# Five modulation vectors as fp32 TensorE products in four column groups, and the first mixer's low parts on one engine

## The chip, the cores and the metric

One NeuronCore of a Trainium2 chip runs the whole program in one launch. The metric is the device time of that launch in microseconds (us), the median of several executions. The engines are TensorE (PE in the profile, its weight loads PEld), VectorE (DVE), ScalarE (ACT), GpSimd (POOL) and SyncE (SP), which here issues nearly all DMAs.

## What is computed

Two transformer blocks in fp32, one behind the other, on 256 tokens of width 2048. What matters here is how a conditioning vector `c` enters: in each block it gives six modulation vectors of 2048 elements (shift, scale and gate for the mixer and for the feed-forward part).

```python
def first_block(x, c, w_ada, b_ada, ...):
    c_act = jax.nn.silu(c)
    mod = c_act @ w_ada[l] + b_ada[l]
    sh_m, sc_m, gt_m, sh_f, sc_f, gt_f = jnp.split(mod[:, None, :], N_MOD, axis=-1)
    h = rmsnorm(x, pre_mix_norm[l]) * (1.0 + sc_m) + sh_m
    proj = h @ w_in[l]
    o_hg = hgrn2_group(...)
    o_gdn = gdn_group(...)
    y = jnp.concatenate([o_hg, o_gdn], axis=-1) @ w_out[l]
    x = x + gt_m * rmsnorm(y, post_mix_norm[l])
    h = rmsnorm(x, pre_ffn_norm[l]) * (1.0 + sc_f) + sh_f
    y = jnp.square(jax.nn.relu(h @ w_ff1[l])) @ w_ff2[l]
    x = x + gt_f * rmsnorm(y, post_ffn_norm[l])
```

`w_ada` is 2048 x 12288 in fp32, so its product with one row is a matter of reading 100 MB for each block. The second block has the same frame with an attention mixer of four kinds and a gated feed-forward part.

## The kernel before

**The stream of weights.** All weight matrices come from HBM in tiles of 512 KB (128 partitions x 1024 fp32), in one list, `items`, in the order in which they are used. `dma_to` issues the DMAs on SP into a ring of `raw` tiles: 5 of them, and 3 more during the prologue. `prep` takes the next item of the list when the planner says so.

**GEMM items.** Products are made at fp32 precision from fp32r parts. ScalarE copies a raw tile to a high part `wh`, and VectorE or GpSimd subtracts it to get the low part `wl` (`low.tensor_tensor` in `prep`; `l_eng` and the item's mark `"low"`, set from the table `LOW`, choose the engine). TensorE then multiplies high x high, high x low and low x high, 12 or 24 products for a tile. There are 4 pairs of `wh`/`wl` (6 in some places), so prepared tiles wait for TensorE there.

**Modulation items.** An item with `"ada"` holds 128 x 1024 elements of `w_ada`: two blocks of 128 rows for one vector, or one block of rows for two vectors. VectorE multiplies each half by the column of `csil` (silu of `c`, one value per partition) and adds it to `acc`, 128 x 512, one instruction for each half:

```python
dve.scalar_tensor_tensor(a, w, sc, a, op0=MUL, op1=ADD)
```

After all 16 row blocks `acc` holds 128 partial sums per column. `col_gen` sums them over the partitions on TensorE, either with four products with `ones`, or with four transposes and four accumulating ScalarE copies, and makes the columns `A` and `B` of a norm. `row_gen` makes a row of a gate with two products with `ones_r`. Vectors 0 and 1 of block 1 (shift and scale of its mixer) are the first things the program needs.

**The order.** The program is written instruction by instruction, in an order that a planner (`_Clock`, with a price for each kind of instruction) works out while it writes; each engine runs its own instructions in that order. `fill`, called after each pair of weight and operand, puts in steps of the generators of the mixer (`fillers`, `pri`, `urgent`) and calls `prep` for the next item if the clock says that its data are there.

**The stages.** A prologue reads the weights of vectors 0 and 1 for the first 512 columns. Then come the eight "wide" blocks of the input product (`hq, hf, hv, hg, zq, zk, zv, gg`, first half of the heads) in three passes over a quarter of the operand each, since each quarter needs its own 512 columns of `A` and `B`. Six of the eight blocks go through two banks of PSUM from the pool `mx` in each pass (`mbanks`) and are added up in SBUF. Then the rest of the input product runs, with the HGRN2 and delta-rule generators in between, and the output product `oA`, `oB`; the feed-forward part; and block 2. The weights of the other modulation vectors are spread between the GEMM items by `weight(k)`. PSUM has eight banks: four for GEMM (`g`), four for everything else (`mx`).

Of the kernel before, what the change touches and what calls it, by code (L numbers as in the profile page):

```python
# [74 lines left out]
class _Clock:  # L75
    """Estimates, while the program is written, when each engine gets to what it is given (us)."""
# [25 lines left out]
    def cost(s, eng, op, out, ins):  # L102
# [3 lines left out]
        if eng == "pe":  # L106
            if op == "transpose":
                return max(n, 128) * 0.417e-3 * 2
            if ins[0].dtype == FR:
                return n * 0.417e-3 * (1 if n >= 256 else 4) + 2.5e-3  # L110
            return 4 * 0.417e-3 * max(n, 128)
# [45 lines left out]
class _Eng:  # L157
    """An engine whose instructions pass through the clock."""
# [18 lines left out]
def two_blocks(ctx, tc, I, out):  # L177
# [57 lines left out]
    def add_ada(blk, v, q, kp, fin, row):  # L235
        items.append({"ada": (blk, v, q, kp), "fin": fin, "row": row})

    def dma_to(n):
        while st["d"] < min(n, len(items)) and rslots:
# [5 lines left out]
            if "ada" in it:  # L245
# [3 lines left out]
                if kp == 0:  # L249
                    for _ in range(40):  # L250
                        if len(accs) + len(vs) > 4:
                            fill_step(True, urgent)
# [16 lines left out]
    def prep(low=None):  # L269
# [9 lines left out]
        if "ada" in it:  # L279
            blk, vs, q, kp = it["ada"]  # L280
            for k in range(2):
# [28 lines left out]

    held = {}
# [23 lines left out]
    def prep_at():  # L335
        """When the data and the place of the next item are there."""
# [172 lines left out]
    def run_last(parts, done, script=()):  # L509
        """Ends of blocks, the first token tile ahead of the second: (block, banks, units)."""  # L510
# [24 lines left out]
    def run_first(b, script, last=False):  # L535
        """A block of kind S at the start of a phase, the first token tile ahead of the second."""
# [122 lines left out]
    def col_gen(blk, v, q):  # L659
# [3 lines left out]
        if blk == 0 and v < 2:  # L663
# [47 lines left out]
    def ada_vecs(blk, vs, key=None, mul=False):  # L711
        n = 8 * len(vs)
        for q in range(4):
            for kp in range(n):
# [6 lines left out]
                ADA.append((blk, vs, q, kp, fin, key is not None))  # L721

# [84 lines left out]
    def turn(post, name):  # L807
        """Steps between two phases: residual sum and norm, (first token tile before the other)."""
# [16 lines left out]
    # =====================================================================  # L825
    # plan of the blocks
    # =====================================================================
# [12 lines left out]
    # ---- evacuations, block 1  # L840
# [80 lines left out]
    # ---- log decay and beta of the delta rule  # L921
# [39 lines left out]
    # ---- gated, normalised heads to the transposed operand  # L961
# [28 lines left out]
    # ---- HGRN2, four heads  # L990
# [56 lines left out]
    # ---- gated delta rule, four heads of one half of the tokens  # L1047
# [153 lines left out]
    # ---- plan of block 1  # L1201
# [107 lines left out]
    # operand tiles of the output product: 0-3, 4-7 first half of the groups, see quad()  # L1309
# [62 lines left out]
    # ---- block 2: evacuations of the input product  # L1372
# [26 lines left out]
    # ---- attention: scores, bias, maximum, exponential and its sum  # L1399
# [155 lines left out]
    # ---- NSA  # L1555
# [142 lines left out]
    # ---- differential attention  # L1698
# [140 lines left out]
    # ---- the modulation's rows come in between, ahead of their uses  # L1839
    ada_vecs(0, (0, 1))  # L1840
    n_first = len(ADA)
    ada_vecs(0, (3, 4))
    ada_vecs(0, (2,), "gt_m", True)
# [10 lines left out]
    def weight(k):  # L1854
        if k[0] in ("oB", "pB") or k == "fv" or k[1:] == (0, 0) and k[0] in ("f1", "ga") or k in (("f1", 0, 1), ("f2", 3, 2), ("f2", 3, 3)):
            return 0.0
        if k == "ab" or k[1] == 0 and k[0] in ("zq", "zk", "zv", "gg", "hq", "hf", "hv", "hg"):
            return 0.3
        if k[0] == "oA":
            return 2.0  # L1860
        if k in ("qG", "kvH", "sv"):
            return 0.5
        if k in (("hq", 1), ("hf", 1)):
            return 0.6
# [148 lines left out]
    while any(it.get("rs", (0,))[0] >= RAW_BUFS for it in items[st["p"]:st["d"]] if "raw" in it):  # L2013
        assert prep()
# [296 lines left out]
```

## Time and profile before

| | us |
|---|---|
| runs of the kernel before | 2861.53, 2865.45, 2865.94 |
| median of the runs | 2865.45 |
| span of the profiled execution (its own time, none other is shown) | 2873.1 |
| TensorE busy | 2634.5 (92%) |
| VectorE busy | 2060.7 (72%) |
| ScalarE busy | 1243.8 (43%) |
| GpSimd busy | 729.0 (25%) |

The mean granted clock of TensorE over the span is 0.959 of 2.4 GHz. The shares are means over stages with different limits, so the rows below are taken by stage: the prologue (0 to 38 us), the three passes of the wide blocks (38 to 249), the rest of the first mixer with `oA` (249 to 790), the turn to the feed-forward part (790 to 857). Nearly all instructions stand on one line of the program, that of the helper `call`, so groups are told apart by the names of their tiles: `acc<-raw,csil,acc` is a multiply-add of a modulation item, `wl<-raw,wh` a low part. An fp32 product of two fp32 operands leaves two records on TensorE.

### The profile page before, as it was taken

To read this page: it belongs to the slowest core of one execution; us is meant where nothing else is said; L and a number is where in the kernel's file an instruction comes from. 1 tells how busy PE (TensorE), PEld (TensorE's weight loads), DVE (VectorE), ACT (ScalarE), POOL (GpSimd) and SP (SyncE) were. 2 spreads that over 40 slices of the span, in tenths; PEclk is the share of its full clock that TensorE was granted. 3 is DMA by queue.
4 is the path that set the end of the run, shared out by engine and by line. 5 is a ranking of instruction groups with operands and counts; after the bars stand their busy time and mean duration, and the time that the engine had idled before them with its cause. 6 is when DMAs were issued, how large, how long until landed. Compare 5 with 4: busy or idle time off the path is not lost.

```text
span 2873.1 us, 43930 instructions
## 1 busy us (share of the span) xinstructions
PE 2634.5 (92%) x17089; PEld 2386.7 (83%) x17089; DVE 2060.7 (72%) x2449; ACT 1243.8 (43%) x2011; POOL 729.0 (25%) x401
## 2 busy tenths in 40 slices
PE   4788889888979999999998899998879999999998
PEld 4778868867869798897997798886669989998997
DVE  7897988899678877778755548678766665554456
ACT  3333343343454444444444436454454444443343
POOL 4663465653130000000002474554520000000001
PEclk9888999889989999999999899999989999999999
DMA  9787566567748988988865675667747777656664
GB/s 319 236 280 193 158 219 198 162 206 239 244 147 271 319 293 291 310 272 303 296 212 166 180 223 168 189 215 249 242 157 228 232 240 229 191 184 191 184 184 146
DMA packets 346593, 643.88 MB, mean 224 GB/s; under 512 B 31488, under 2 KB 50640, under 8 KB 344976
## 3 DMA queue, kind: packets, MB, share of 16 engines
q1 hardware_dynamic: 343296, 628.26, 68.4%
q10 hardware_dynamic: 2336, 10.42, 1.0%
q8 instruction: 134, 2.20, 0.3%
q0 software_dynamic: 752, 2.39, 0.2%
q14 instruction: 75, 0.61, 0.1%
HBM read 636.27 MB, written 4.19 MB: 223 GB/s over the span
## 4 chain that ended last, share of the span: by engine, by line
PE 49%; DVE 8%; DMA 6%; ACT 3%; issue 3%; POOL 2%; SPq 0%; ACTq 0%; POOLq 0%; DVEq 0%
PE g L167 47%; DMA raw<-in_w_ff_dram 5%; DVE acc L167 2%; PE mx L167 2%; DVE wl L167 2%; ACT wh L167 2%; POOL wl L167 1%; DMA raw<-in_ada_w_dram 1%; DVE xres L167 1%; POOL y L167 1%; DVE S L167 0%; DVE hTl L167 0%; ACT hTh L167 0%; DVE v L167 0%; ACT sq L167 0%
## 5 line engine op out<-in xcount | busy, mean ns | idle before, releaser
L167 ACT ACTIVATE wh<-raw 128x1024 fp32r<-128x1024 f32 (+2 forms) x817 | 846.6, 1045 | 1072.0 <-PE g L167 554.7
L167 DVE TENSOR_TENSOR wl<-raw,wh 128x1024 fp32r<-128x1024 f32 (+1 forms) x601 | 751.2, 1256 | 487.5 <-ACT wh L167 479.2
L167 PE MATMUL g<-hTh,wh 128*128 128x256 f32 x3328 | 961.0, 289 | 5.3 <-ACT wh L167 2.5
L167 PE MATMUL g<-hTh,wl 128*128 128x256 f32 x3328 | 950.8, 286 | 6.5 <-POOL wl L167 5.0
L167 PE MATMUL g<-hTl,wh 128*128 128x256 f32 x3328 | 949.3, 285 | 0.3 <-DVE hTl L167 0.3
L167 DVE SCALAR_TENSOR_TENSOR acc<-raw,csil,acc 128x512 f32<-128x512 f32 x736 | 732.6, 1020 | 77.1 <-DMA raw<-in_ada_w_dram 59.2
L167 PEld LDWEIGHTS g<-hTh,wh 128*128 128x128 f32 x3328 | 644.3, 194 | 11.9 <-issue 4.7
L167 PEld LDWEIGHTS g<-hTh,wl 128*128 128x128 f32 x3328 | 643.1, 193 | 8.0 <-POOL wl L167 5.6
L167 PEld LDWEIGHTS g<-hTl,wh 128*128 128x128 f32 x3328 | 645.6, 194 | 1.6 <-DVE hTl L167 0.6
L167 POOL TENSOR_TENSOR wl<-raw,wh 128x1024 fp32r<-128x1024 f32 (+3 forms) x216 | 529.7, 2461 | 415.6 <-ACT wh L167 395.2
L167 POOL TENSOR_TENSOR y<-y,gw 128x512 f32<-128x512 f32 x22 | 32.0, 1474 | 1291.0 <-ACT sq L167 733.1
L167 PE MATMUL g<-wh,rh 128*128 128x512 f32 x864 | 340.2, 394 | 0.0
L167 PE MATMUL g<-wl,rh 128*128 128x512 f32 x864 | 339.5, 393 | 0.0
L167 PE MATMUL g<-wh,rl 128*128 128x512 f32 x864 | 339.5, 393 | 0.0
L167 PEld LDWEIGHTS g<-wh,rl 128*128 128x128 f32 x864 | 162.9, 189 | 36.3
L167 PEld LDWEIGHTS g<-wl,rh 128*128 128x128 f32 x864 | 163.0, 189 | 35.7
L167 PEld LDWEIGHTS g<-wh,rh 128*128 128x128 f32 x864 | 162.9, 189 | 35.5
L167 PE MATMUL g<-wh,hTh 128*128 128x512 f32 (+3 forms) x344 | 138.8, 403 | 18.1 <-ACT hTh L167 12.7
L167 PE MATMUL g<-wl,hTh 128*128 128x512 f32 (+3 forms) x344 | 131.6, 383 | 11.8 <-DVE wl L167 6.9
L167 PE MATMUL g<-wh,hTl 128*128 128x512 f32 (+3 forms) x344 | 131.4, 382 | 0.1
L167 PEld LDWEIGHTS g<-wh,hTh 128*128 128x128 f32 x344 | 69.2, 201 | 31.2 <-ACT hTh L167 15.5
L167 PEld LDWEIGHTS g<-wl,hTh 128*128 128x128 f32 x344 | 69.2, 201 | 24.5 <-DVE wl L167 8.9
(455 smaller groups left out, 2790.2 us busy)
## 6 DMA issues: line engine op xcount, KB each, us to landing
raw<-in_w_ff_dram SPq DMA_DIRECT2D x256, 512.0 KB
raw<-in_w_ada_dram SPq DMA_DIRECT2D x192, 512.0 KB
raw<-in_ada_w_dram SPq DMA_DIRECT2D x192, 512.0 KB
raw<-in_w_in_dram SPq DMA_DIRECT2D x176, 512.0 KB
raw<-in_ffn_w_gate_dram SPq DMA_DIRECT2D x88, 512.0 KB
raw<-in_ffn_w_up_dram SPq DMA_DIRECT2D x88, 512.0 KB
raw<-in_ffn_w_down_dram SPq DMA_DIRECT2D x88, 512.0 KB
raw<-in_w_out_dram SPq DMA_DIRECT2D x60, 512.0 KB
```

The lines of the kernel that those rows point to most:

```text
L167: r = f(out, *a, **kw)
```

## The change

- Vectors 0, 1, 2, 3 and 4 of block 1 (mark `cg`) are no longer summed on VectorE. Two items make four products: a column of `csil`, repeated 32 times, is the stationary operand, and the 128 x 512 of the raw tile are the moving one. The four write partitions 0 to 31, 32 to 63, 64 to 95 and 96 to 127 of one bank of PSUM, `ada`; over 8 items the bank collects all 16 row blocks, every sum standing in 32 equal rows. `ada_cg` then copies it to `acc` on ScalarE with a factor of 1/32 (for the gate row, VectorE adds it to `acc`). The rest of the way is as before; `col_gen` uses products with `ones` for all of block 1.
- The five vectors' items now hold one vector each; `ADA` is ordered so that vectors 0 and 1 alternate in runs of eight. Items go into the stream in pairs.
- Every low part up to the end of the first mixer is on VectorE: the entries of block 1 in `LOW` are gone, and the wide blocks have the mark 0 instead of 3 (3 chose by the clock).
- `weight` has no special shares for the first mixer's blocks any more.
- One bank of PSUM goes from `mx` (now 3) to `ada` (1), for the whole program.
- The planner's price for the new products is 0.25 us; this sets the order alone.

```diff
@@ class _Clock: cost
         if eng == "pe":
+            if op == "matmul" and out.shape[0] == 32 and n == 512:
+                return 0.25
@@ prep
         if "ada" in it:
             blk, vs, q, kp = it["ada"]
+            if it["cg"]:
+                return ada_cg(it)
...
+    def ada_cg(it):
+
+        blk, (v,), q, kp = it["ada"]
+        cgs.setdefault("held", []).append(it)
+        if kp % 2:
+            if kp == 1:
+                cgs["p"] = ps["a"].tile([128, 512], F32, name="ada", tag="ada")
+            p = cgs["p"]
+            for j in range(4):
+                i = cgs["held"][j // 2]
+                kt = blk * 16 + 2 * i["ada"][3] + j % 2
+                mm(p[32 * j:32 * j + 32], csil[:, kt:kt + 1].to_broadcast([128, 32]),
+                   i["raw"][:, (j % 2) * 512:(j % 2 + 1) * 512], kp == 1, kp == 7)
+            for i in cgs.pop("held"):
+                del i["raw"]
+                if i["rs"][0] < st["r"]:
+                    rslots.append(i["rs"])
+        if kp == 7:
+            if it["row"]:
+                a = accs[blk, v, q]
+                dve.scalar_tensor_tensor(a, p, 1 / 32, a, op0=MUL, op1=ADD)
+            else:
+                room(1)
+                a = accs[blk, v, q] = accp.tile([128, 512], F32, name="acc", tag="acc")
+                act.activation(a, p, AF.Copy, scale=1 / 32)
+            it["fin"]()
+        return True
@@ col_gen
-        if blk == 0 and v < 2:
+        if blk == 0:
@@ plan
-    ada_vecs(0, (0, 1))
+    for v in (0, 1):
+        ada_vecs(0, (v,), cg=True)
+    ADA[:] = [ADA[32 * v + 8 * q + i] for q in range(4) for v in range(2) for i in range(8)]
     n_first = len(ADA)
-    ada_vecs(0, (3, 4))
-    ada_vecs(0, (2,), "gt_m", True)
+    for v in (3, 4):
+        ada_vecs(0, (v,), cg=True)
+    ada_vecs(0, (2,), "gt_m", True, cg=True)
@@ weight
-        if k == "ab" or k[1] == 0 and k[0] in ("zq", "zk", "zv", "gg", "hq", "hf", "hv", "hg"):
-            return 0.3
-        if k[0] == "oA":
-            return 2.0
...
-        if k in (("hq", 1), ("hf", 1)):
-            return 0.6
...
-    LOW.update({**{(n, h): 1 for n, h in (("zq",0),("zk",0),("zq",1),("zk",1),("zv",1))}, **{(n,h):2 for n,h in (("zv",0),("gg",0),("hq",1),("hf",1),("hv",1),("hg",1),("gg",1))}})
...
                 b.idx.append(add_w(*u))
-                items[-1]["low"] = 3
-                for _ in range((1, 2)[len(b.idx) % 2]):
+                items[-1]["low"] = 0
+                for _ in range(2 if len(b.idx) % 2 or b in (wide[0], wide[3]) else 0):
                     if nxt:
                         add_ada(*nxt.popleft())
...
                 while ai < ntot and (ai - a0) < na * done / tot:
-                    add_ada(*ADA[ai])
-                    ai += 1
+                    for _ in range(1 + ADA[ai][6]):
+                        add_ada(*ADA[ai])
+                        ai += 1
@@ run
-    ps["m"], close_m = opener("psm", None, bufs=4, space=PSUM)
+    ps["m"], close_m = opener("psm", None, bufs=3, space=PSUM)
+    ps["a"], close_a = opener("psa", None, bufs=1, space=PSUM)
```

Written out, the program has 320 new products on TensorE; on VectorE 304 multiply-adds and 16 first products on modulation weights fewer, 95 low parts more and 4 additions from `ada`; on ScalarE 16 copies from `ada` and 32 accumulating copies fewer; on GpSimd 95 low parts fewer. The number of DMAs is the same.

How this moves instructions shows on VectorE in the second pass of the wide blocks, before `hv` is added up (`Bmix`, `colt` and `Amix` make the columns for the next quarter of the operand). Before:

```order
L167 SCALAR_TENSOR_TENSOR acc<-raw,csil,acc 128x512 x12
L167 TENSOR_TENSOR hv<-mx,hv 128x512 x2
L167 SCALAR_TENSOR_TENSOR acc<-raw,csil,acc 128x512 x4
L167 TENSOR_TENSOR hg<-mx,hg 128x512 x2
L167 SCALAR_TENSOR_TENSOR acc<-raw,csil,acc 128x512 x4
L167 TENSOR_TENSOR Bmix_123<-mx,cols 128x4
L167 TENSOR_TENSOR part<-mx,part 128x512 x2
L167 TENSOR_TENSOR colt<-mx,cols 128x4
```

And with the change:

```order
L169 TENSOR_TENSOR wl<-raw,wh 128x1024
L169 TENSOR_TENSOR Bmix_123<-mx,cols 128x4
L169 TENSOR_TENSOR wl<-raw,wh 128x1024 x5
L169 TENSOR_TENSOR hv<-mx,hv 128x512 x2
L169 TENSOR_TENSOR wl<-raw,wh 128x1024
L169 TENSOR_TENSOR colt<-mx,cols 128x4
L169 SCALAR_TENSOR_TENSOR Amix_122<-colt,cols 128x4
```

The multiply-adds ahead of the evacuations of `mx` are low parts now, and `Bmix` and `colt` come earlier.

On TensorE, in the rest of the first mixer, the products of the HGRN2 generator (`hq,hk`) stand between those of a GEMM block. Before, one such place reads:

```order
L167 MATMUL g<-hTh_178,wl 128x256
L167 MATMUL mx<-hq,hk 128x64 x8
L167 MATMUL g<-hTh_178,wh 128x256
L167 MATMUL g<-hTl_182,wh 128x256
L167 MATMUL g<-hTh_178,wl 128x256
```

With the change, in the same generator:

```order
L169 MATMUL g<-wh,hTl_183 128x512
L169 MATMUL mx<-hq,hk 128x64 x8
L169 MATMUL ada<-raw,csil 32x512 x4
L169 MATMUL g<-wh,hTh_179 128x512
L169 MATMUL g<-wl,hTh_179 128x512
```

The four products of two modulation items stand in TensorE's own order, ahead of the GEMM products that follow.

On GpSimd the stretch from the first low part to the end of the first HGRN2 steps reads before:

```order
L167 TENSOR_TENSOR r_118<-r_118,mhalf 128x2
L167 TENSOR_TENSOR wl<-raw,wh 128x1024 x46
L167 CAST mk_1962<-x 128x896
L167 CAST mk_1963<-x 128x896
L167 TENSOR_TENSOR wl<-raw,wh 128x1024 x4
L167 TENSOR_TENSOR hk<-hk,hf 128x512
L167 TENSOR_TENSOR hk<-hk,hf 128x256x2
L167 TENSOR_TENSOR wl<-raw,wh 128x1024
L167 TENSOR_TENSOR hk<-hk,hf 128x128x4
```

And with the change:

```order
L169 TENSOR_TENSOR r_118<-r_118,mhalf 128x2
L169 CAST mk_1994<-x 128x896
L169 CAST mk_1995<-x 128x896
L169 TENSOR_TENSOR hk<-hk,hf 128x512
L169 TENSOR_TENSOR hk<-hk,hf 128x256x2
L169 TENSOR_TENSOR hk<-hk,hf 128x128x4
```

All low parts are gone from GpSimd there; what is left are the steps of the generators.

## Rows read from the trace of the kernel before

**Rows 1.** The page, first line

```profile
span 2873.1 us, 43930 instructions
```

**Rows 2.** Windows: stretch, us, busy (xcount) of PE, PEld, DVE, ACT, POOL; PEclk, DMA, GB/s

```profile
0.00:38.00 38.00, 7.49 (x28) 5.75 (x28) 23.06 (x37) 10.31 (x15) 12.18 (x27) 1.00 0.99 357
38.00:249.00 211.00, 170.98 (x1011) 156.27 (x1012) 183.94 (x183) 70.01 (x87) 121.61 (x46) 0.87 0.80 246
249.00:640.00 391.00, 342.81 (x2349) 313.82 (x2348) 343.08 (x435) 163.74 (x377) 216.97 (x114) 0.93 0.62 191
640.00:790.00 150.00, 131.23 (x713) 112.02 (x713) 119.71 (x168) 62.50 (x104) 34.93 (x26) 0.93 0.74 241
...
857.00:1500.00 643.00, 635.37 (x4127) 579.95 (x4126) 495.37 (x580) 283.42 (x390) 0.00 (x0) 0.99 0.85 287
1600.00:2140.00 540.00, 483.61 (x3216) 429.35 (x3215) 375.12 (x508) 265.50 (x562) 277.78 (x144) 0.94 0.64 202
```

**Rows 3.** TensorE's waits in 38 to 249: us in total, times, longest us

```profile
PE mx L167 <- DVE acc L167: 19.2, 3, 9.4
PE mx L167 <- POOL wl L167: 8.2, 7, 1.8
```

**Rows 4.** TensorE's waits in 249 to 790

```profile
PE g L167 <- DVE wl L167: 16.3, 6, 6.0
PE mx L167 <- DVE hgA L167: 15.0, 8, 5.5
PE mx L167 <- DVE gdP L167: 8.7, 6, 3.9
```

**Rows 5.** Groups by line in 38 to 249: busy us, mean ns, idle before

```profile
L167 DVE SCALAR_TENSOR_TENSOR acc<-raw,csil,acc 128x512 f32<-128x512 f32 x90 | 126.4, 1469 | 5.5 <-DMA raw<-in_w_ada_dram 5.5
...
L167 POOL TENSOR_TENSOR wl<-raw,wh 128x1024 fp32r<-128x1024 f32 x45 | 121.1, 2702 | 82.7 <-ACT wh L167 82.6
```

**Rows 6.** The same in 249 to 857

```profile
L167 DVE SCALAR_TENSOR_TENSOR acc<-raw,csil,acc 128x512 f32<-128x512 f32 x184 | 203.0, 1132 | 3.8 <-DMA raw<-in_w_ada_dram 2.3
```

**Rows 7.** The same in 857 to 1500

```profile
L167 DVE TENSOR_TENSOR wl<-raw,wh 128x1024 fp32r<-128x1024 f32 x221 | 269.6, 1224 | 115.7 <-ACT wh L167 110.3 <-PE g L167 2.6
...
L167 DVE SCALAR_TENSOR_TENSOR acc<-raw,csil,acc 128x512 f32<-128x512 f32 x244 | 177.5, 748 | 7.6 <-DMA raw<-in_ada_w_dram 4.1 <-DMA raw<-in_w_ada_dram 1.2
```

**Rows 8.** The SP queue's waits in 38 to 249

```profile
SPq L167 <- DVE acc L167: 93.5, 41, 13.8
```

**Rows 9.** The SP queue's waits in 249 to 790

```profile
SPq L167 <- DVE acc L167: 140.5, 65, 7.5
```

**Rows 10.** Timeline of TensorE near 400: start us, us, what

```profile
399.57 1.02 PE L167 MATMUL mx<-gdM,c 128*128 128x512 f32 x2
400.43 0.60 PE L167 MATMUL mx<-c,zq 128*128 128x128 f32 x4
```

**Rows 11.** Timeline of TensorE near 1764

```profile
1762.80 0.28 PE L167 MATMUL g<-hTl,wh 128*128 128x256 f32 x1
1762.92 0.28 PE L167 MATMUL g<-hTh,wl 128*128 128x256 f32 x1
1763.13 0.65 PE L167 MATMUL mx<-PcT,vcb 128*64 128x256 f32 x2
...
1764.27 0.43 PE L167 MATMUL mx<-PcT,vcb 128*64 128x256 f32 x1
1764.48 0.38 PE L167 MATMUL mx<-S,sv 128*64 128x256 f32 x1
...
1764.70 1.52 PE L167 MATMUL mx<-S,sv 128*64 128x128 f32 x10
1766.15 0.39 PE L167 MATMUL g<-hTh,wh 128*128 128x256 f32 x1
```

**Rows 12.** ScalarE's waits in 38 to 249, then in 249 to 790

```profile
ACT wh L167 <- DMA raw<-in_w_in_dram: 57.0, 23, 6.9
...
ACT wh L167 <- DMA raw<-in_w_in_dram: 64.2, 27, 6.9
```

More of the change, by code (lines that the diff above doesn't have):

```diff
@@ L233, in add_w, with add_ada, room @@
         return len(items) - 1
-    def add_ada(blk, v, q, kp, fin, row):
-        items.append({"ada": (blk, v, q, kp), "fin": fin, "row": row})
+    def add_ada(blk, v, q, kp, fin, row, cg):
+        items.append({"ada": (blk, v, q, kp), "fin": fin, "row": row, "cg": cg})
+    def room(n):
+        for _ in range(40):
+            if len(accs) + n > 4:
+                fill_step(True, urgent)
     def dma_to(n):
@@ L248, in dma_to @@
                 w = adas[blk][0]
[L249 to L252, printed above, removed]
+                if kp == 0 and (it["row"] or not it["cg"]):
+                    room(len(vs))
                     for v in vs:
@@ L308, in prep @@
             rslots.append(it["rs"])
+        return True
+    cgs = {}
+    def ada_cg(it):
[23 more added lines that the diff above has]
+            it["fin"]()
         return True
@@ L709, in two_blocks, with ada_vecs @@
     ADA = []
-    def ada_vecs(blk, vs, key=None, mul=False):
+    def ada_vecs(blk, vs, key=None, mul=False, cg=False):
         n = 8 * len(vs)
@@ L720, in ada_vecs @@
                         fin = lambda q=q: urgent.append((clk.wr[clk.key(accs[blk, vs[0], q])][0] + 0.2, row_gen(blk, vs[0], q, key, mul)))
-                ADA.append((blk, vs, q, kp, fin, key is not None))
+                ADA.append((blk, vs, q, kp, fin, key is not None, cg))
     def rsq(dst, src, scale, n, eng=dve):
@@ L2012, in two_blocks @@
             b.first = 12
-    while any(it.get("rs", (0,))[0] >= RAW_BUFS for it in items[st["p"]:st["d"]] if "raw" in it):
+    while any(it.get("rs", (0,))[0] >= RAW_BUFS for it in items[st["p"]:st["d"]] if "raw" in it) or cgs.get("held"):
         assert prep()
@@ L2274, in two_blocks @@
     close_y()
+    close_a()
     close_m()
```

## The prediction

> **What bounds the kernel now.** I read the windows table first [rows 2]. From 857 to 1500 us TensorE is busy 635 of 643 us at clock 0.99: nothing but TensorE work can be saved there. The two stretches of the first mixer are different. In 38 to 249 (the eight wide blocks, three passes) TensorE is idle 211 - 171.0 = 40.0 us, at a mean clock of 0.87; in 249 to 790 (rest of the first mixer) it is idle 48.2 + 18.8 = 67.0 us, clock 0.93. VectorE is busy 183.9 of 211 and 463 of 541 us there, and GpSimd 121.6 and 252. A clock of 0.87 means that 26% of the stretch ran at 1.2 GHz instead of 2.4 (each cold us does half the work); taking TensorE busy in it, the clock cost 27 us, and 38 us in the second stretch. So idle plus cold is 67 us in the first and 105 us in the second: this is the pool from which anything can be won. [Rows 3, 4] say who holds TensorE. In the first stretch the longest is DVE acc, 19.2 us in three waits (the end of a modulation vector, without which no operand exists for the next pass), then GpSimd's low parts; in the second it is VectorE under several names (wl 16.3, hgA 15.0, gdP 8.7).
>
> Why VectorE is late shows in the cost of one multiply-add: 1469 ns in the first stretch, 1132 in the second, but 748 in 857 to 1500, where GpSimd does nothing [rows 5 to 7] (its column in [rows 2]). The same instruction takes twice as long while GpSimd's subtractions of 2702 ns run. The late multiply-adds also hold the weight ring: the DMA queue on SP waited 93.5 us and 140.5 us for DVE acc to give back a raw tile [rows 8, 9].
>
> **What the change removes.** Of 768 VectorE instructions on modulation weights 320 go (304 multiply-adds and 16 first products). 128 of them lie before 249 us, 32 of these before 38 us; so 96 in the first stretch, and 192 in the second. At the two mean prices VectorE loses about 126 + 7 us (90 multiply-adds; the first products are the rest) and 203 + 4 us. 95 low parts move from GpSimd to VectorE: 45 in the first stretch and 50 in the second, at 1224 ns (the price with GpSimd silent [rows 7]) 55 and 61 us. VectorE then stands at 184 - 133 + 55 = 106 of 211, and 463 - 207 + 61 = 317 of 541 us: 50% and 59% instead of 87% and 86%. Neither GpSimd nor VectorE can be the bound there afterwards. Both are covered by TensorE, so by themselves they save nothing; what they save is TensorE's waits.
>
> **What it adds on TensorE.** 320 fp32 products of 128 x 32 by 512 columns, in 80 groups of four; 8 groups lie in the first 38 us, which wait for DMA anyway and cost nothing; 24 lie in the first stretch and 48 in the second, mostly alone between other products. One fp32 product of 512 columns on the whole array is two records that take 0.86 us from 399.57 to 400.43 [rows 10]. A group therefore costs between 0.86 us (all four side by side) and 3.44 us (one after another). The nearest row is the attention's value product of block 2, fp32 too, whose 64-column halves are written one head after the other: PcT,vcb, then four S,sv, for head 0, and then the same for head 1. [Rows 11] show head 1's PcT,vcb starting at 1764.27, before head 0 is through (its last products start after 1764.48): 20 records (twelve of 256 columns, eight of 128) last from 1763.13 to 1766.15, 3.02 us; one after the other, at the 0.43 us per 512 columns of [rows 10], they would need 12 x 0.215 + 8 x 0.107 = 3.44. So column groups do run side by side, with some delay. The entry also costs: from 1762.92 to 1763.13 is 0.21 instead of 0.12 us, so about 0.1 us, and I take the same for the exit. Per group I choose 1.2 us: near the lower end, since the overlap is seen, plus 0.2 of entry and exit and 0.15 for one straggler. Ends kept: 1.06 and 3.64 us. TensorE thus gets 24 x 1.2 = 29 us and 48 x 1.2 = 58 us.
>
> The stretches as sums. First: 171 - 27 = 144 us of work at full clock, + 29, + idle and cold. Of the 67 us, the causes acc, POOL wl and the late evacuations go; left are late DMA, the hand-over of operands and the ring of banks (below). I leave 20: 193 instead of 211, **-18 us**. (The DMA allows it: 246 GB/s over 211 us is 52 MB, 145 us at the 357 GB/s of the first 38 us.) Second: 474 - 38 = 436 + 58 + 35 left of 105 = 529 instead of 541, **-12 us**. I leave a third, since the chains hgA and gdP are made of short waits that a less busy VectorE shortens but does not end. With the best end (1.06 us, 10 and 20 us left) it is -32 and -34; with the dearest group and nothing won, +60 and +137.
>
> The rest. The 16 evacuations on ScalarE (it is busy 70 of 211 us) and 4 on VectorE cost nothing unless a group stands behind one: all use one bank, but two groups of neighbouring vectors lie apart. The 32 transposes with 32 accumulating ScalarE copies fewer, and 32 products with ones more, are a few us each way beside other work. The 160 tiles of weights are the same DMAs of 512 KB on SP, now one vector to a tile; with the block weights gone they are spread evenly up to oA instead of gathering in it (0.74 of the DMA there against 0.62 before it [rows 2]), which costs nothing as long as both shares stay under the 0.99 of the first 38 us. **The bank**: mx has three instead of four to the very end. In the wide passes each block takes two; its second is then the first of the block before, which VectorE or ScalarE must have emptied, 0.68 us plus at most one low part of 1.22, against the 0.7 us until TensorE needs it: 0 to 1.2 us for each of 18 turns, which I count in the 20 us above. In block 2's mixer (1600 to 2140, TensorE busy 484 of 540 [rows 2]) nothing changes but this bank. No row gives its price: 0 below, and above, the 56 us of idle there half as much again, 28. I take 6, since those waits are mostly for data, not for banks. **+6 us.**
>
> Sum: -18 - 12 + 6 = -24 us. The profiled execution's own time is its span of 2873.1 us [rows 1], 7.65 us above the median of the runs, 2865.45; the difference is carried over. 2865.5 - 24 gives **2841 us**.
>
> **Rivals.**
> *Column groups in program order* (slower). If a product may not start before the one ahead of it has, a group is a staircase: the second record of each product waits for its first, and the next product for that. Eight records in five steps of 0.43 us make 2.15, with entry 2.35 us, 1.15 more than mine; 72 groups, +83 us: 2924. It turns the sign from 1.5 us a group (24 / 72 = 0.33 more). [Rows 11] speak against it, since head 1's first record starts before records that precede it in the program. The Trainium skill, "TensorE: Matmul & The Clock Gate", Part 3, states just this rule: matmuls keep program order in start and end, and a weight load overlaps running matmuls only when its row group differs. By that rule the trace disagrees, there on columns 64 wide. Four in full succession (+176 us, 3017) I count here too. 0.10.
>
> *TensorE stands behind a late weight tile* (slower). Until now a late modulation tile held only VectorE, and TensorE had four prepared weight tiles to go on with. Now the products stand in TensorE's own order, and whatever GEMM is behind them waits too. ScalarE, which meets its tiles at about the same place in the program, waited for DMA 57.0 us in 23 waits and 64.2 in 27 [rows 12]: 2.4 us each. If half of the 72 pairs of tiles meet such a wait, 36 x 2.4 = 86 us; as the queue no longer waits 234 us for DVE acc, I halve it: +43, together +19, 2884 us. It decides from 10 pairs (10 x 2.4 = 24 us). For: the ring is only 5 tiles deep after the prologue, and a pair holds two. Against: DMA was late because VectorE returned tiles late. 0.14.
>
> *The bank eats it*. If block 2's mixer loses 28 us instead of 6, 2863: no change. 0.10.
>
> *The change does not do what it says*: excluded, as its written order of instructions shows the 320 products and the moved low parts.
>
> **Numbers.** Forecast 0.66, with a range of its own from 2865 - 32 - 34 = 2799 to some 2856; rivals 0.10 (order), 0.14 (late tile), 0.10 (bank). About 0.2% (5.7 us) is what a measurement of this kernel can tell from no change: faster 0.66, same 0.10, slower 0.24. For 8 in 10 the range goes from 2795 (4 us below the best end, for a turn between the stages that gains a little) up to 2886, which takes in the bank and the late tile's own value, and leaves the staircase out.
>
> **What would show it.** Right: multiply-adds on modulation weights only after 790 us, near 0.75 us; GpSimd without wl before 790; four ada records pairs within about 1.0 us, second column group starting within 0.1 us of the first; the wide passes ending near 230 instead of 249, and the feed-forward part (857) near 827; DVE acc gone from TensorE's waits. Wrong: groups of 2 us and more; TensorE waits on the DMA of modulation weights over 25 us in sum; TensorE idle in 1600 to 2140 grown by more than 15 us; GpSimd's removal leaving VectorE's instructions as slow as before.

## The result, and the profile after

The changed kernel takes 2885.77 us (median of 7 runs, 2877.46 to 2893.85), the kernel before 2868.22 beside it: ratio 1.0057, 95% interval 1.0034 to 1.0081. It is slower by 0.6% where I forecast it faster by 0.8%. The profiled span grew from 2873.1 [rows 1] to

```profile
span 2883.8 us, 44820 instructions
```

The windows of the changed kernel, cut at the same events as those of before [rows 2] (stretch, us, busy (xcount) of PE, PEld, DVE, ACT, POOL; PEclk, DMA, GB/s):

```profile
0.00:40.00 40.00, 19.70 (x93) 6.69 (x93) 2.11 (x7) 11.40 (x18) 8.98 (x26) 0.87 0.99 359
40.00:276.00 236.00, 198.43 (x1216) 151.87 (x1216) 92.22 (x130) 73.82 (x92) 0.56 (x1) 0.91 0.75 226
276.00:795.00 519.00, 507.06 (x3448) 415.52 (x3449) 287.17 (x463) 220.63 (x419) 108.78 (x88) 1.00 0.65 207
795.00:866.00 71.00, 55.30 (x244) 42.97 (x243) 49.79 (x67) 42.53 (x80) 29.38 (x21) 0.88 0.43 139
866.00:1500.00 634.00, 627.39 (x4100) 573.82 (x4099) 491.79 (x577) 280.98 (x388) 0.00 (x0) 1.00 0.86 289
1606.00:2150.00 544.00, 487.42 (x3211) 431.50 (x3210) 385.10 (x507) 266.12 (x560) 278.69 (x145) 0.94 0.63 200
```

The wide passes end where GpSimd makes the masks (`mk<-x`): 248.5 us before, 275.4 now. Read against the forecast:

| stretch | before, us | after, us | forecast, us |
|---|---|---|---|
| prologue | 38 | 40 | 38 |
| wide passes | 211 | 236 | 193 |
| from there to the feed-forward part | 608 | 590 | 596 |
| block 2's mixer | 540 | 544 | 546 |

So the rest of the first mixer did better than I said, the bank in block 2 about what I said, and the wide passes are 25 us longer instead of 18 shorter. Who holds TensorE there is in its waits from 40 to 276 (us in total, times, longest):

```profile
PE mx L169 <- DVE part L169: 13.7, 6, 2.3
PE mx L169 <- DVE hg L169: 8.2, 2, 4.1
PE mx L169 <- ACT x L169: 5.3, 4, 2.9
PE mx L169 <- DVE hv L169: 4.7, 2, 2.3
PE mx L169 <- ACT part L169: 2.5, 3, 0.8
PE mx L169 <- ACT hg L169: 1.8, 1, 1.8
```

DVE acc and POOL wl [rows 3] are gone, as forecast. In their place stand `part`, `hg` and `hv`, 30.9 us. TensorE does not read these; it waits for the bank of `mx` that they are copied out of (an evacuation). One such wait, on all three engines (timeline; in brackets the idle time before and what ended it):

```profile
144.61 1.06 ACT L169 ACTIVATE wh<-raw 128x1024 fp32r<-128x1024 f32 x1 [2.88 <-PE mx L169]
...
144.87 0.39 PE L169 MATMUL mx<-wh,hTl 128*128 128x512 f32 x1
...
145.70 1.22 DVE L169 TENSOR_TENSOR wl<-raw,wh 128x1024 fp32r<-128x1024 f32 x1 [2.71 <-ACT wh L169]
...
146.84 1.28 DVE L169 TENSOR_TENSOR hv<-mx,hv 128x512 f32<-128x512 f32 x2
...
147.58 0.50 PE L169 MATMUL mx<-wh,hTh 128*128 128x512 f32 x1 [2.33 <-DVE hv L169]
```

ScalarE can make the next high part only when TensorE gives back a weight slot; VectorE's low part waits for that high part; and the evacuation of `hv` stands behind this low part in VectorE's queue although its data were ready at about 145.3 (144.87 + 0.39). VectorE is idle most of the stretch (busy 92 of 236 us) and still late. Eight of the ten waits for VectorE's `part`, `hg` and `hv` are like this one, 2.26 to 2.33 us behind a low part for whose high part VectorE had stood idle. The other two, 4.1 us each, are `hg`, behind a low part and the eight steps that make the next quarter of the operand. The largest cause of VectorE's waits from 40 to 276, and then of ScalarE's, say the same:

```profile
DVE wl L169 <- ACT wh L169: 130.3, 40, 8.4
```

```profile
ACT wh L169 <- PE mx L169: 103.6, 32, 7.1
```

### The profile page after: what moved, and what is told of

Read it like the earlier page. It is cut to its first block, busy times and chain, and to the rows that moved or that the text cites. A ratio compares the mean times of both kernels' runs of the same rounds, so it can differ in the third digit from the quotient of the medians.

```text
span 2883.8 us, 44820 instructions
## 1 busy us (share of the span) xinstructions
PE 2713.4 (94%) x17761; PEld 2377.2 (82%) x17761; DVE 1783.3 (62%) x2228; ACT 1246.2 (43%) x1963; POOL 464.1 (16%) x306
## 4 chain that ended last, share of the span: by engine, by line
PE 52%; DVE 7%; DMA 5%; issue 3%; ACT 3%; POOL 2%; SPq 0%; ACTq 0%; POOLq 0%; DVEq 0%
PE g L169 50%; DMA raw<-in_w_ff_dram 3%; PE mx L169 3%; DVE acc L169 2%; DVE wl L169 2%; ACT wh L169 1%; DMA raw<-in_ada_w_dram 1%; POOL wl L169 1%; DVE xres L169 1%; POOL y L169 1%; DMA raw<-in_w_in_dram 0%; DVE S L169 0%; ACT sq L169 0%; DVE y L169 0%; ACT hTh L169 0%
## 5 line engine op out<-in xcount | busy, mean ns | idle before, releaser
L169 DVE TENSOR_TENSOR wl<-raw,wh 128x1024 fp32r<-128x1024 f32 x696 | 871.8, 1258 | 720.6 <-ACT wh L169 713.3
L169 PEld LDWEIGHTS g<-hTh,wh 128*128 128x128 f32 x3328 | 637.8, 192 | 42.9 <-issue 36.0
L169 DVE SCALAR_TENSOR_TENSOR acc<-raw,csil,acc 128x512 f32<-128x512 f32 x432 | 391.9, 919 | 64.3 <-DMA raw<-in_ada_w_dram 57.7
L169 POOL TENSOR_TENSOR wl<-raw,wh 128x1024 fp32r<-128x1024 f32 (+3 forms) x121 | 275.8, 2288 | 236.4 <-ACT wh L169 232.3
L169 PE MATMUL ada<-raw,csil 128*32 128x512 f32 x640 | 107.7, 645 | 16.5 <-DMA raw<-in_w_ada_dram 14.7
```

Of the source, the lines that this page charges most:

```text
L169: r = f(out, *a, **kw)
```

## The experiments

Theory **Order**: an evacuation stands on VectorE behind a low part that waits for TensorE, and only with three banks does this hold TensorE. Theory **Bank**: three banks alone do it. Theory **Groups**: the products cost TensorE more than I priced. All ratios are to the kernel before, with 95% intervals; a difference "by the ratios" is the difference of two ratios times 2868 us. Names that start with `a_` are versions of the changed kernel, those with `b_` versions of the kernel before.

### The halves of the change alone

The bank alone (`b_bank3`):

```diff
-    ps["m"], close_m = opener("psm", None, bufs=4, space=PSUM)
+    ps["m"], close_m = opener("psm", None, bufs=3, space=PSUM)
```

> The kernel before with three banks in mx instead of four, nothing else. Theory Order (in the changed kernel an evacuation of mx stands on VectorE behind a low part that waits for a weight slot, and only together with three banks does this hold TensorE): here evacuations stand behind multiply-adds of 1.5 us that wait for nothing of TensorE, so the bank costs little, 0 to 12 us, 2868 to 2880, with some 5 of it in block 2's mixer. Theory Bank (three banks alone do it): the wide passes end 20 to 30 us later than in the kernel before and the run is at 2890 or more.

2893.06 us, ratio 1.0084 (1.0064 to 1.0104): the bank alone costs some 24 us, twice what Order allowed. Bank's time is met but not its reason: the wide passes end at 259 us, 10 later than before and not 20 to 30. TensorE's waits from 38 to 250 hold the same three names without any product on `ada` and without a waiting low part:

```profile
PE mx L167 <- DVE part L167: 17.7, 4, 6.3
PE mx L167 <- DVE hv L167: 14.4, 2, 7.8
PE mx L167 <- DVE hg L167: 9.0, 2, 6.6
```

Here it is the multiply-adds, and at a pass's end the steps that make the next quarter of the operand, that stand ahead of the evacuations.

The low parts alone, in the kernel before (`b_low`):

```diff
-    LOW.update({**{(n, h): 1 for n, h in (("zq",0), ...
...
-                items[-1]["low"] = 3
+                items[-1]["low"] = 0
```

> The kernel before with all low parts of the first mixer on VectorE (four banks, modulation on VectorE as before). If GpSimd's work is what makes a multiply-add take 1.13 to 1.47 us instead of 0.75, VectorE pays 55 + 61 us of low parts and gets back 90 x 0.72 + 184 x 0.38 = 135 us, so it is no busier than before, multiply-adds stand at 0.75 to 0.85 us and the time stays within 15 us of the kernel before, 2855 to 2885. If multiply-adds are slow for another reason (their DMA, their own ports), they stay above 1.1 us and VectorE holds TensorE for 60 us or more: above 2920.

2806.16 us, ratio 0.9786 (0.9738 to 0.9833): 62 us faster, which neither side expected. VectorE from 38 to 250, and the windows of the wide passes and of the rest of the first mixer:

```profile
L167 DVE TENSOR_TENSOR wl<-raw,wh 128x1024 fp32r<-128x1024 f32 x60 | 73.3, 1227 | 16.1 <-ACT wh L167 15.9
L167 DVE SCALAR_TENSOR_TENSOR acc<-raw,csil,acc 128x512 f32<-128x512 f32 x98 | 68.0, 743 | 0.0
```

```profile
39.00:208.00 169.00, 154.95 (x1008) 143.03 (x1008) 150.39 (x224) 68.31 (x83) 1.52 (x2) 0.96 0.91 308
208.00:720.00 512.00, 461.96 (x3052) 415.40 (x3051) 420.28 (x652) 223.31 (x475) 114.23 (x87) 0.95 0.67 214
```

The multiply-add falls from 1469 [rows 5] to 743 ns once GpSimd makes no low parts, and the wide passes end at 206 instead of 249 us. The slow multiply-adds were GpSimd's doing, and to silence GpSimd is nearly all that any version here wins.

The other way round, the changed kernel with the marks of before (`a_low`):

```diff
+    LOW.update({**{(n, h): 1 for n, h in (("zq",0), ...
...
-                items[-1]["low"] = 0
+                items[-1]["low"] = 3
```

> The changed kernel with the first mixer's low parts shared with GpSimd again, by the marks of the kernel before. Theory Order: evacuations no longer stand behind waiting low parts, TensorE's waits for mx in the wide passes fall below half of the 32 us, but GpSimd's low parts (2.7 us each) are waited for by some 10 us and slow VectorE; net 5 to 20 us faster than the changed kernel, 2865 to 2880. Theory Groups or Bank: low parts have no part in it, and the slower low parts make it 5 to 15 us slower, 2890 to 2900.

2872.93 us, ratio 1.0008 (0.9984 to 1.0031), as Order said; TensorE's waits for `hg` and `part` in the wide passes are 14.5 us where those for `hg`, `part` and `hv` were 30.9, and these passes end at 255 instead of 275 us. The stretch behind them takes some 12 us longer, so that by the ratios the low parts on VectorE cost 14 us in the changed kernel; in the kernel before they are worth 61. The parts of the change work against each other.

### The order of the evacuations

In the wide passes the evacuations of a block are written right after its last product, ahead of the next tile's preparation and of the steps for the next quarter (`a_evac`):

```diff
-                fill()
+                if tail or kk < it["nk"] - 1 or i != idx[-1]:
+                    fill()
...
+                if end:
+                    if q:
+                        add_acc(b, pts, b.acc)
+                    else:
+                        act.activation(b.acc[0], pts[0], AF.Copy)
+                        dve.tensor_copy(b.acc[1], pts[1])
+                    fill()
```

> The changed kernel with one difference in order: in the wide passes a block's evacuations of mx are written ahead of the next weight tile's preparation (and ahead of the steps that make the next quarter of the operand) instead of behind it. Theory Order: TensorE's waits for hv, hg and part (32 us before 276) fall below 12 us, the cold clock that follows them shrinks, the wide passes end 25 to 40 us earlier, and the run is at 2850 to 2862. Theory Groups (the four products cost TensorE more than was priced, and waits only move): the wide passes end at most 8 us earlier, 2877 or more. Theory Bank: the waits halve at best, 2868 to 2877.

2838.69 us, ratio 0.9911 (0.9883 to 0.9939): some 42 us faster than the changed kernel by the ratios, more than Order said, and faster than the kernel before. The windows:

```profile
40.00:232.00 192.00, 183.10 (x1216) 141.31 (x1215) 96.06 (x132) 75.40 (x92) 0.15 (x1) 0.97 0.89 275
232.00:752.00 520.00, 508.47 (x3450) 416.66 (x3451) 284.97 (x462) 219.69 (x418) 109.56 (x88) 0.99 0.64 207
```

The waits for `part`, `hg` and `hv` are gone altogether (5.0 us for `ACT x` is the longest cause left), and the wide passes take 192 us, the 193 of my sum. Of the 44 us, 29 are TensorE's idle time (37.6 before this edit, 8.9 with it) and 15 its clock: the same 1216 records are busy 198.43 us at 0.91 and 183.10 at 0.97. The second stretch does not move (519 and 520).

The same order in the kernel before (`b_evac`):

> The kernel before with the evacuations of the wide passes written first, low parts and banks as before. TensorE waits only 7.9 us there for part and hv, and no low part stands ahead of the evacuations on VectorE: 0 to 8 us faster, 2858 to 2868. If the order alone were worth what it is in the changed kernel (47 us), below 2840.

2870.26 us, ratio 1.0018 (0.9994 to 1.0042): no gain. The 42 us belong to what the changed kernel has besides: its bank and its low parts.

Three runs separate bank and order where VectorE makes all low parts of the first mixer and all modulation: three banks (`b_low_bank3`), the new order (`b_low_evac`), and both (`b_low_evac_b3`).

> The kernel before with all low parts of the first mixer on VectorE and three banks in mx. With the kernel before's low parts the bank alone cost 25 us. Theory Bank (the price of the bank is that of evacuations that stand behind other work of VectorE, whatever it is): 15 to 30 us more than with four banks, 2821 to 2836. Theory Contention (it was dear only since GpSimd slowed VectorE): under 10 us more, below 2816.

> The kernel before with all low parts of the first mixer on VectorE, and in the wide passes a block's evacuations written ahead of the next tile's preparation. With four banks TensorE waits only some 8 us there for part and hv. If these waits were all that is left for the order to win, 2797 to 2806 against the 2806 of the low parts alone. If the order matters as much as with three banks (47 us), below 2780.

> The kernel before with all low parts of the first mixer on VectorE, the evacuations of the wide passes written ahead of the next tile's preparation, and three banks in mx. Theory Order (the bank is dear only where an evacuation stands behind a low part that waits for TensorE): the bank costs 5 to 20 us instead of 51, some 5 of them in block 2, so 2804 to 2819, and the products of the changed kernel cost what is left to its 2839 with the same order, 20 to 35 us. Theory Bank (a spare bank is needed whatever the order): 2835 or more.

Three banks: 2857.0 us, 0.9955 (0.9941 to 0.997), 48 us above b_low by the ratios and far above either expectation. New order: 2799.25, 0.9755 (0.9738 to 0.9772), the lowest time here, but its interval overlaps that of b_low: a gain over b_low is not shown. Both: 2817.89, 0.9842 (0.9811 to 0.9872), so with evacuations first the bank costs 25 us by the ratios (0.0087; the medians are 19 apart), about what Order said or a little more. The two traces are 15 us apart: 5 of these lie in the wide passes, which end at 210 instead of 206 us, and 9 in the rest of the first mixer, where the cause stays open. TensorE's waits from 38 to 255 in `b_low_bank3`:

```profile
PE mx L167 <- DVE part L167: 15.3, 6, 3.7
PE mx L167 <- DVE hv L167: 10.5, 2, 5.3
PE mx L167 <- DVE hg L167: 4.6, 2, 2.3
```

Seven of these ten waits are of 2.3 us, behind a low part for whose high part VectorE had stood idle, and the wide passes end at 253 instead of 206 us. Neither theory holds alone: the bank costs some 25 us behind multiply-adds or with evacuations first, and twice that behind low parts that wait for TensorE.

### The products

Groups made twice (`a_dbl`):

> The changed kernel with each of the 48 groups of vectors 2, 3 and 4 made twice (the sum is then halved once more at the evacuation): 48 groups of four products more, nothing else. Theory Groups (TensorE is the bound there, so a group costs its whole time on TensorE, 0.9 to 1.3 us): 43 to 62 us more than the changed kernel, 2929 to 2948. Theory Cover (a group falls into time in which TensorE would wait): under 20 us more, below 2906.

```diff
+            for j in range(4 if v > 1 else 0):
+                i = cgs["held"][j // 2]
...
+                   i["raw"][:, (j % 2) * 512:(j % 2 + 1) * 512], False, kp == 7)
```

2916.78 us, ratio 1.0176 (1.0151 to 1.0202): 34 us by the ratios (31 by the medians) for 48 groups more, between the two expectations. One group in the changed kernel, then a doubled one (timeline of TensorE; x8 is eight records in one line):

```profile
425.71 0.28 PE L169 MATMUL g<-hTh,wl 128*128 128x256 f32 x1
425.92 1.06 PE L169 MATMUL ada<-raw,csil 128*32 128x512 f32 x8
426.92 0.39 PE L169 MATMUL g<-hTh,wh 128*128 128x256 f32 x1
427.14 0.28 PE L169 MATMUL g<-hTl,wh 128*128 128x256 f32 x1
```

```profile
409.00 1.92 PE L169 MATMUL ada<-raw,csil 128*32 128x512 f32 x16
410.85 0.39 PE L169 MATMUL g<-hTh,wh 128*128 128x256 f32 x1
```

A group holds TensorE for 1.00 us, with 0.09 before it (0.21 instead of 0.12) and 0.10 behind it (0.22 instead of 0.12): 1.19 us. A second one behind it adds 0.85 (1.85 from start to start). 48 x 0.85 = 41 us, of which 7 to 10 did not show; that they fell into time in which TensorE would have waited is argued and not shown. Record by record, the four first records of the group start at 425.920 to 425.940 and the four second ones at 426.374 to 426.393. Of the 46 groups from 276 to 795 us, 32 hold TensorE for 0.99 to 1.09 us. In the other 14 the second of the two tiles came late and its pair of products ran behind the first pair, up to 3.2 us in all; the mean is 1.29.

Vectors 0 and 1 back on VectorE, evacuations first (`a_cg342`):

```diff
-    for v in (0, 1):
-        ada_vecs(0, (v,), cg=True)
-    ADA[:] = ...
+    ada_vecs(0, (0, 1))
```

> The changed kernel with the evacuations written first, and vectors 0 and 1 on VectorE as in the kernel before; vectors 2, 3 and 4 stay on TensorE, three banks. Theory Groups (TensorE is the bound in the wide passes too once it does not wait for banks): 26 groups of 1.2 us go, 31 us, VectorE pays 96 multiply-adds of 0.75 us and is busy some 175 of 195 us, and the run is 15 to 30 us faster than with all five, 2809 to 2824. Rival (with three banks the multiply-adds ahead of the evacuations hold TensorE again, as in the kernel before with three banks): 2839 to 2865.

2843.12 us, ratio 0.9919 (0.989 to 0.9948): no different from a_evac. The wide passes end at 223 instead of 232 us, 9 us for 24 groups that went (2 of the 26 there belong to vector 3); TensorE waits for banks again (`hv` 8.9 us, `part` 3.8, `hg` 3.2). The result lies in the rival's range, but the multiply-adds are not all of it: `b_low_evac_b3`, with the same multiply-adds, order and number of banks, has its wide passes through at 210. What else differs there, the spread of the items above all, was not tested alone.

The spread of the modulation items as before, with the old order of evacuations (`a_oldw`) and with the new (`a_evac_oldw`), and the even spread in the version with the lowest time (`b_low_evac_w`, which takes the same lines out of the kernel before):

```diff
+        if k == "ab" or k[1] == 0 and k[0] in ("zq", "zk", "zv", "gg", "hq", "hf", "hv", "hg"):
+            return 0.3
+        if k[0] == "oA":
+            return 2.0
...
+        if k in (("hq", 1), ("hf", 1)):
+            return 0.6
```

> The changed kernel with the spread of the modulation items over the first mixer's blocks as before (few in the first half, double shares in the output product). Theory Spread (the even spread is part of what the change costs, as it cost 25 us where VectorE sums): 10 to 25 us faster than the changed kernel, 2861 to 2876. Theory Groups (on TensorE a group costs the same wherever it stands, and nothing there waits for VectorE any more): within 6 us of the changed kernel, 2880 to 2892; slower, if raw tiles gather in front of the output product and groups wait for their DMA.

> The same with the evacuations of the wide passes written first. Theory Spread: 2814 to 2829. Theory Groups: within 6 us of the 2839 with the even spread, so that what is left between it and the 2818 of three banks without products is TensorE's time for the products.

> The kernel before with all low parts of the first mixer on VectorE and the evacuations of the wide passes written first, and with the changed kernel's even spread of the modulation items over the blocks of the first mixer: no products on TensorE, four banks. In the version without the spread the DMA's share is 0.42 at 300 to 400 us and VectorE is busy 65 of 100 us there, and 49 of 50 at 600 to 650. If the old shares were made for a VectorE that GpSimd slowed, an even spread gives 5 to 15 us, 2785 to 2795 against 2799. Rival: the generators between the blocks need VectorE more than the multiply-adds do, and their chains get longer: 2800 to 2815.

With products on TensorE the spread is worth nothing that can be measured: 2884.07 (1.0064, 1.0038 to 1.009) and 2833.63 (0.9898, 0.9866 to 0.9931). Where VectorE sums, the even spread costs 1.0%: 2824.25 (0.9856, 0.9838 to 0.9874). There 57 us of multiply-adds lie between 205 and 400 us instead of 35, and TensorE's waits for VectorE's `wl` from the wide passes to the feed-forward part go from 17.4 to 34.8 us.

Between a_evac (0.9911) and three banks without products (b_low_evac_b3, 0.9842) stand 20 us. The windows of b_low_evac_b3, cut at the same events as those of a_evac above:

```profile
40.00:210.00 170.00, 152.14 (x1008) 139.19 (x1009) 152.12 (x227) 69.55 (x83) 0.00 (x0) 0.97 0.92 309
210.00:731.00 521.00, 468.19 (x3048) 419.41 (x3047) 418.48 (x649) 223.14 (x475) 115.31 (x88) 0.94 0.66 209
```

The wide passes take 170 us against 192: that is where the 20 us lie. The stretch behind takes 521 against 520. The engines' busy time on the pages of a_evac and then of b_low_evac_b3:

```profile
PE 2696.2 (95%) x17761; PEld 2362.3 (83%) x17761; DVE 1783.4 (63%) x2228; ACT 1247.5 (44%) x1963; POOL 464.6 (16%) x306
```

```profile
PE 2612.6 (93%) x17089; PEld 2363.4 (84%) x17089; DVE 1984.8 (71%) x2544; ACT 1244.9 (44%) x2011; POOL 471.4 (17%) x306
```

TensorE is busy 84 us more with the products, VectorE 201 less. 12.7 of the 84 lie in the prologue, 31.0 in the wide passes and 40.3 in the stretch behind, where they made nothing longer: TensorE is idle 53 of 521 us there without them and 12 of 520 with them. In the wide passes the products' own time is the likely cause, but it is not shown alone: without 24 of the 26 groups a_cg342 wins only 9 of the 22 us.

### The bank later, and GpSimd later

The fourth bank back after the first mixer, evacuations first (`a_evac_b4`; every fourth tile of `mx` then takes it):

```diff
+    close_a()
+    ps["x"], close_a = opener("psx", None, bufs=1, space=PSUM)
```

> The changed kernel with the evacuations written first, and with the fourth bank of mx back once the last of its modulation products is through (after the output product oA of the first mixer). If the bank costs in block 2's mixer what the two traces differ by there, 4.6 us, this gives 2832 to 2836 against 2839; if the mixer's waits for S (16 us) all come from the bank, 2823 to 2829; if those 4.6 us were chance, 2837 to 2841.

2832.64 us, ratio 0.9897 (0.9872 to 0.9922). Against a_evac (0.9911) that is 4 us, as expected in size, but inside both intervals, so it is not shown. TensorE's waits for `S` from 1560 to 2105 are shorter, first without and then with the bank:

```profile
PE mx L169 <- DVE S L169: 15.9, 13, 4.9
```

```profile
PE mx L169 <- DVE S L169: 10.5, 5, 4.9
```

All low parts of block 2 on VectorE too, on top of b_low (`b_low_all`):

```diff
-    LOW = {k: 1 for k in ("qG", "kvH", ...
+    LOW = {}
```

> The kernel before with all low parts on VectorE, those of block 2's mixer and output product too (107 fewer on GpSimd there). If GpSimd's subtractions are what makes VectorE slow, multiply-adds in block 2's mixer fall from 1.21 to near 0.75 us, VectorE goes from 375 to some 425 of 538 us there, TensorE's waits for GpSimd (8.6 us) go, and the run is 5 to 15 us faster than with the first mixer alone, 2791 to 2801. Rival: VectorE's longer queue delays the softmax steps on which the mixer's end hangs, and it is 0 to 20 us slower, 2806 to 2826.

2819.2 us, ratio 0.9828 (0.981 to 0.9846): 0.4% above b_low, with intervals that overlap, so that a loss is not shown; the gain that was expected did not come. In block 2's mixer the multiply-add does fall, from 1207 to 756 ns; what holds TensorE is now mainly

```profile
PE g L167 <- ACT wh L167: 18.1, 8, 4.8
PE mx L167 <- DVE S L167: 13.0, 6, 6.4
```

against 4.2 and 8.1 us in b_low. ScalarE's `S` steps wait 24.0 us for VectorE's `ns` instead of 15.0. Why ScalarE is late stays open; a faster instruction was not enough here.

## Why the prediction was wrong, step by step

By the ratios, times 2868 us, and taken in this order, the change divides so: low parts to VectorE -61 us (1 to 0.9786), the bank on top of that +48 (to 0.9955), products in place of multiply-adds, with all that goes with them, +29 (to 1.0057): together +16. In another order the parts have other prices: the bank alone costs 24, and with evacuations first the products cost 20.

**The step that failed** is the term of the bank in the wide passes: "0.68 us plus at most one low part of 1.22, against the 0.7 us until TensorE needs it: 0 to 1.2 us for each of 18 turns, which I count in the 20 us above". The evacuation does not stand behind one low part that is free to run. It stands behind one whose high part waits for the slot that TensorE gives back at the end of that block: 1.06 us of ScalarE and 1.22 of VectorE, one after the other, before it starts, and at a pass's end behind the operand steps too (4.1 us for `hg`). Taking the order away took 44 us off the stretch (236 to 192), 2.4 us for each of 18 turns, twice my upper end; 15 of the 44 are the lower clock, which my price of a turn left out. In the terms of the sum, the 20 us set for idle and cold time became 59: 37.6 idle, and 21 by the clock of 0.91 (18% of 236 us at half speed). In a_evac they are 15 (8.9 and 6). The hand-over stood in my own rows: the low parts of 857 to 1500 come behind 115.7 us of idle time, 110.3 of it ended by ACT wh [rows 7]. I priced the busy time ahead of the evacuation and not what the instruction ahead of it waits for. With 44 us more my sum of -24 becomes +20; by the spans it was +10.7, the difference being mostly what the rest of the first mixer won beyond my forecast (6 us) and the feed-forward part, 3 us shorter.

**VectorE's relief**: right as such. Multiply-adds stand only behind 790 us, at 747 ns, and GpSimd has no low part before. VectorE is busy 39% and 55% (50% and 59% forecast). But how busy VectorE is was not what held TensorE afterwards.

**The group of four**: right where its tiles are there, 1.2 us chosen and 1.19 measured; with the 14 groups whose second tile was late the mean from 276 to 795 is 1.29 and the same 0.19, some 1.5. The rival of program order is out: the group above has no staircase of five steps, as all four first records start within 20 ns. The Trainium skill, "TensorE: Matmul & The Clock Gate", Part 3, has matmuls in strict order in start and end, and applied to single records that gives the staircase. Record by record this trace disagrees, as [rows 11] did on columns 64 wide, since the first product's second record starts at 426.374, behind the first record of the fourth at 425.940; of the four products as wholes it says nothing against that order.

**The rest of the first mixer**: right in sign, too careful in size: -18 to the feed-forward part instead of -12. At clock 1.00 TensorE is idle 12 of 519 us, where I left 35 us idle and cold. But the mechanism was another: b_low, without any product and with VectorE still busy 420 of 512 us, needs 512 us there as well, so what shortened this stretch was GpSimd's silence and not a VectorE with less to do. **The even spread costs nothing**: right here, but only because the products had left VectorE. **The bank in block 2**: 6 us forecast, 540 to 544 us in the traces; a_evac_b4 gives 4 us too, but inside the intervals.

**The late weight tile**: too large, but not nothing. TensorE waits 8.0 us for modulation tiles from 276 to 795, and the 14 groups that came apart hold it some 14 us longer than whole ones: together some 20 us, not 43. That its 2884 is close to the result is chance. **The bank eats it** was the right resource, with too little of it and in the wrong stage: I looked for it in block 2.

**What I missed besides**: I read in [rows 5 to 7] that GpSimd doubles the multiply-add's price, and then let the products have the credit. The sum took 133 and 207 us of multiply-adds off VectorE and added the low parts; it never asked what the low parts alone would do. In b_low, with multiply-adds at 743 ns, VectorE is busy 150 of 169 us in the wide passes and holds TensorE there for under 10 us. The products then solve a problem that hardly exists any more, for 80 x 1.19 = 95 us of TensorE's time, by this estimate, and a bank. A smaller slip: the ends of "+60 and +137" for "nothing won" keep the idle time but not the 27 and 38 us of cold clock; with these they are +87 and +175.

## What to carry to other kernels

Price the parts of a change apart before adding them up: if one part removes the cause of a stall, the other parts are left with their costs alone. Before a PSUM bank is given up, look at what the instruction ahead of each evacuation waits for, not at how long it runs; an engine that is idle 60% of the time can still be late because of its order. Writing the evacuation ahead of the next preparation was worth 42 us in the changed kernel and 32 in b_low with three banks, and nothing that these runs can tell with four.

## What the runs showed of the hardware

The slowing of VectorE by GpSimd depends on the operands. In the kernel before, from 38 to 249 us, an evacuation with one operand in PSUM is as fast as in b_low (677 and 679 ns), while multiply-adds, both of whose large operands lie in SBUF, take twice as long (1469 [rows 5] and 743 ns):

```profile
L167 DVE TENSOR_TENSOR part<-mx,part 128x512 f32<-128x512 f32 x14 | 8.9, 677 | 0.0
```

The Trainium skill, "SBUF — State Buffer", section "Who interferes with whom", says that a VectorE instruction with two SBUF inputs contends with a GpSimd instruction that reads SBUF, and that one with at most one, outside the modes that use two ports, does not. These rows agree: GpSimd's subtraction reads two SBUF tiles [rows 5].
